# A low part by an adding DMA: how the FFN's last weights are split in two

## The chip, the cores and the metric

One core of a Trainium2 chip runs the whole kernel. The metric is the device time of one execution in microseconds; the time of a kernel is the median over runs.

## The reference

One layer of a streaming encoder on 512 tokens of width 1024, all in float32: RMSNorm, one wide projection, chunked attention with 16 heads beside a gated linear recurrence, a gated merge, then the feed-forward part and a last norm. The change sits in the last product of the feed-forward part:

```python
hn = rmsnorm(h, norm_ffn_g[l])
gu = hn @ w_ffn_in[l]                          # 1024 -> 2 x 2816
g, up = jnp.split(gu, 2, axis=-1)
h = h + (jax.nn.silu(g) * up) @ w_ffn_out[l]   # 2816 -> 1024
return rmsnorm(h, final_norm_g)
```

## The kernel before

The kernel multiplies in float32r (fp32r in the profile), so every float32 operand is split into a high part, which is the operand rounded to that format, and a low part, which is the operand minus the high part. A product is then three matmuls (`mm3`, lines 70 to 72): high by high, high by low, low by high. The split of a tile of weights is done by `split` (lines 76 and 77): ScalarE copies `raw` into the high part, VectorE subtracts the high part from `raw`. GpSimd does the subtraction in a few places only (lines 206, 839 and others).

Weights come in chunks, in an order that `plan` writes out. `load` issues a chunk's transfers from SP's queue into buffers tagged `raw`, each of 512 KB (128 partitions x 1024 float32); three of them rotate. `prefetch` splits each into a tile `hl` (named `whl_<chunk>` in the profile), which holds both parts; `weights(name, ahead)` makes that chunk and the next `ahead` of them. The chunks of `w_ffn_out` are named `fo<half>_<k0>`: two halves of the output columns (512 each), six chunks of rows each, five of 4x128 rows and a last one of 2x128. A chunk of 4 row blocks needs two tiles, the last one a single tile, so there are 22 tiles in all. Their `whl` buffers rotate in two groups of four: two chunks in the pool `wp`, which the earlier weights use too, then two in the pool `op` that is opened for this stage.

The feed-forward input projection (`fg` and `fu` chunks) is a Strassen-like product, `block_product`, whose last call is `fu20`; it prefetches `fo0_0`. Then, for the first half of the columns, the loop walks over chunks, and in each over the four blocks of 128 tokens (`out_tile`, four results side by side). The activations are split by `split_act` on the way, its low parts on GpSimd for pairs 0, 1, 2 and 4 and on VectorE for the others. The second half does the same for its first four chunks; its last two chunks are walked token block by token block, with the closing norm of each block behind it.

```python
wf = weights(f"fo{cc}_{k0}", 3)
for (t, at), po in zip(pieces, pos):
    out_tile(t, po, k0, wf, at)
```

The program gives the instructions in one order, and a planner that estimates durations at build time settles the order within each engine's queue. Each engine runs its own queue strictly in that order and waits on semaphores.

Of the kernel before, what the change touches and what calls it, by code (L numbers as in the profile page):

```python
# [10 lines left out]
AF = mybir.ActivationFunctionType  # L11
ALU = mybir.AluOpType
# [24 lines left out]
def block_kernel(ctx: ExitStack, tc: tile.TileContext, x, norm_mix_g, w_in, b_merge, rel_table,  # L37
# [3 lines left out]
    pe, dve, act, pool, sp = nc.tensor, nc.vector, nc.scalar, nc.gpsimd, nc.sync  # L41
# [20 lines left out]
    def f(ap):  # L62
        return ap.bitcast(F32)
# [10 lines left out]
    def split(hi, lo, src):  # L74

        act.activation(hi, src, AF.Copy)  # L76
        dve.tensor_sub(lo, src, f(hi))  # L77
# [55 lines left out]
    def load(name, k):  # L133
        _, parts, rows, kts = chunks[index[name]]
        wide = sum(width for *_, width in parts)
        n = min(4 * CW // wide, kts - k)
        at = rows + k * P
        pl, bufs = wp, 3
        if name in strassen and name[0] == "f":
            loads[0] += 1  # L140
            pl, bufs = (room[0], 1) if loads[0] % 4 == 0 else (wp, 3)
        raw = pl.tile([P, n, wide], F32, tag="raw", bufs=bufs, name=f"raw_{name}_{k}")
        to = 0
        for src, col, width in parts:
            sp.dma_start(out=raw[:, :, to:to + width],
                         in_=src[at:at + n * P, col:col + width].rearrange("(k p) e -> p k e", p=P))
            to += width
        raws[name, k] = raw
# [5 lines left out]
    def weight_sums(name):  # L154

        for k in (0, 4):
            if (name, k) not in raws:
                load(name, k)
        r0, r1 = raws.pop((name, 0)), raws.pop((name, 4))
        a11, a21, a12, a22 = r0[:, :, 0:P], r0[:, :, P:CW], r1[:, :, 0:P], r1[:, :, P:CW]  # L160
        sc = room[0]
        s21, s34 = (sc.tile([P, 2, 4, P], F32, tag=tag, bufs=1, name=f"{tag}_{name}")
                    for tag in ("s21", "s34"))
        s2, s1, s3, s4 = s21[:, 0], s21[:, 1], s34[:, 0], s34[:, 1]
        dve.tensor_add(s1, a21, a22)
        dve.tensor_sub(s2, s1, a11)
        other = pool if name in ("fg2", "fu2", "fg4") else dve
        other.tensor_sub(s3, a11, a21)
        other.tensor_sub(s4, a12, s2)
        blocks_ = {}  # L170
        for group in ((("a11", a11), ("a12", a12)), (("s2", s2), ("s1", s1)), (("s3", s3), ("s4", s4)), (("a22", a22),)):
            pl, tag, bufs = sc, "a22", 2
            if len(group) == 2:
                slots[0] += 1
                pl, tag, bufs = (sc, "whl", 1) if slots[0] % 5 == 0 else (wp, "whl", 4)
            o = pl.tile([P, len(group), 2, 4, P], F32R, tag=tag, bufs=bufs, name=f"whl_{name}_{group[0][0]}")
            together = group[0][0] in ("s2", "s3") and name != "fg2"
            if together:
                split(o[:, :, 0], o[:, :, 1], (s21 if group[0][0] == "s2" else s34)[:])
            for i, (key, src) in enumerate(group):  # L180
                if not together:
                    split(o[:, i, 0], o[:, i, 1], src)
                blocks_[key] = o[:, i]
        return blocks_

    def prefetch(n):
        while len(made) < min(n, len(chunks), index.get(barrier[0], len(chunks))):
            name, parts, rows, kts = chunks[len(made)]
            if name in strassen:
                made.append(weight_sums(name))  # L190
                continue
            tiles = []
            wide = sum(width for *_, width in parts)
            step = 4 * CW // wide
            for k in range(0, kts, step):
                n_ = min(step, kts - k)
                if name in extra:
                    hl = extra[name].tile([P, 2, n_, wide], F32R, tag="whl", bufs=4, name=f"whl_{name}_{k}")
                else:
                    hl = wp.tile([P, 2, n_, wide], F32R, tag="whl", bufs=4, name=f"whl_{name}_{k}")  # L200
                if (name, k) not in raws:
                    load(name, k)
                raw = raws.pop((name, k))
                if len(made) == 0 and k:
                    act.activation(hl[:, 0], raw[:], AF.Copy)
                    pool.tensor_sub(hl[:, 1], raw[:], f(hl[:, 0]))
                else:
                    split(hl[:, 0], hl[:, 1], raw[:])
                tiles.append(hl)
            made.append(lambda part, k, at, tiles=tiles, step=step: tiles[k // step][:, part, k % step, at])  # L210

    def weights(name, ahead=1):
        prefetch(index[name] + 1 + ahead)
        return made[index[name]]
# [70 lines left out]
    for name, w in (("r", w_rg_r), ("i", w_rg_i)):  # L285
        raw = nm.tile([P, 8, P], F32, name=f"wrg_raw_{name}")
# [146 lines left out]
    for name, raw in zip("ri", wrg_raw):  # L433
        hl = rw2.tile([P, 2, 8, P], F32R, bufs=1, name=f"wrg_{name}")
# [305 lines left out]

    hsq = []
    prefetch(index["wo1"] + 1)
    for t in range(NT):
        q2 = cp.tile([P, 2], F32, tag="hsq2", bufs=2, name=f"hsq2_{t}")
# [75 lines left out]
    room[0] = sc  # L820
    barrier[0] = "fo0_16"
    prefetch(index["fg2"] + 1)

    for i, name in enumerate(("fg0", "fg0", "fu0", "fu0")):
# [129 lines left out]
```

## Time and profile before

| | |
|---|---|
| median of 2 runs | 901.03 us (900.98 to 901.07) |
| the profiled execution | 900.88 us |
| its span | 899.1 us |
| mean granted TensorE clock | 0.993 |
| TensorE (PE) busy | 881.4 us |
| VectorE (DVE) busy | 553.6 us |
| ScalarE (ACT) busy | 473.5 us |
| GpSimd (POOL) busy | 133.1 us |

The span is what the profile covers; the execution's time has 1.8 us around it. A row of a group gives the line of the program, the engine, the operation, what is written and read, the number of instructions, their busy time in us and the mean of one in ns, then the idle time of that engine just ahead of them and what ended most of it. `SPq` is SP's queue, which issues DMAs.

### The profile page before, as it was taken

What the parts mean: (1) busy time and instruction counts of PE and PEld (TensorE: products, weight loads), DVE (VectorE), ACT (ScalarE), POOL (GpSimd) and SP (SyncE); (2) the same over time, 40 slices, a digit from 0 to 9 for tenths busy, and PEclk for the clock granted to TensorE, in tenths of its full rate; (3) what the DMA queues carried; (4) which work ended last, traced back from release to release, by engine and by line L of the source; (5) the groups of instructions that cost most, each with busy time, mean ns of one, the idle gap of its engine ahead of it and who ended that gap; (6) DMA issues with size and microseconds to landing.
All of it is one profiled execution on the core that took longest, in us unless ns stands there. A gap on an engine that the chain in (4) does not pass through costs nothing.

```text
span 899.1 us, 13343 instructions
## 1 busy us (share of the span) xinstructions
PE 881.4 (98%) x5220; PEld 778.1 (87%) x5220; DVE 553.6 (62%) x863; ACT 473.5 (53%) x841; POOL 133.1 (15%) x168
## 2 busy tenths in 40 slices
PE   8999999999999999999999999899999999999997
PEld 5988888888888889797888889899999999888886
DVE  5776556553466676666546455998888887453203
ACT  7566546642257666666533365556555556623103
POOL 4012112120023222222100002510000001300100
PEclk9999999999999999999999999899999999999999
DMA  8323222423332232331123620333433333353002
GB/s 261 95 71 117 85 84 90 118 94 94 105 104 73 74 111 64 93 95 60 66 63 124 217 66 30 117 117 95 140 96 94 96 118 108 98 184 120 30 1 94
DMA packets 85023, 89.05 MB, mean 99 GB/s; under 512 B 5344, under 2 KB 73552, under 8 KB 84960
## 3 DMA queue, kind: packets, MB, share of 16 engines
q1 hardware_dynamic: 83584, 84.73, 30.7%
q10 hardware_dynamic: 1376, 3.47, 1.1%
q8 instruction: 41, 0.67, 0.3%
q14 instruction: 22, 0.18, 0.1%
HBM read 86.05 MB, written 2.14 MB: 98 GB/s over the span
## 4 chain that ended last, share of the span: by engine, by line
PE 92%; DVE 3%; ACT 2%; issue 1%; DMA 1%; POOL 1%; SPq 0%; DVEq 0%; ACTq 0%; POOLq 0%
PE po_out L70 5%; PE po_out L72 5%; PE po_out L71 5%; PE p_fu L71 2%; PE p_fu L70 2%; PE p_fu L72 2%; PE p_fg L72 2%; PE p_fg L71 2%; PE p_fg L70 2%; PE o L659 2%; PE po_ga L70 2%; PE pT L639 2%; PE po_ga L71 2%; PE po_ga L72 2%; PE po_ya L70 2%; PE po_ya L71 2%
## 5 line engine op out<-in xcount | busy, mean ns | idle before, releaser
L70 PE MATMUL po_out<-whl_fo,act_hi 128*128 128x512 f32 (+1 forms) x198 | 73.2, 369 | 0.0
L71 PE MATMUL po_out<-whl_fo,act_hi 128*128 128x512 f32 (+1 forms) x198 | 72.9, 368 | 0.0
L72 PE MATMUL po_out<-whl_fo,act_lo 128*128 128x512 f32 (+1 forms) x198 | 72.1, 368 | 0.0
L77 DVE TENSOR_TENSOR whl_fo<-raw_fo,whl_fo 128x1024 fp32r<-128x1024 f32 x22 | 27.5, 1259 | 47.0 <-ACT whl_fo L76 47.0
L627 POOL TENSOR_SCALAR p<-p,rl 128x128 f32<-128x128 f32 (+1 forms) x64 | 37.4, 605 | 84.4 <-DVE rl L625 83.8
L76 ACT ACTIVATE whl_fo<-raw_fo 128x1024 fp32r<-128x1024 f32 x22 | 23.0, 1056 | 50.6 <-PE po_out L72 36.1
L624 ACT ACTIVATE p<-p,m 128x128 f32<-128x128 f32 (+3 forms) x64 | 35.5, 555 | 22.0 <-DVE m L623 21.6
L623 DVE CUSTOM_DVE_ANT_0 p<-s,bias 128x128 f32<-128x128 f32 (+3 forms) x64 | 29.8, 487 | 22.6 <-PE s L621 21.8
L72 PEld LDWEIGHTS po_out<-whl_fo,act_lo 128*128 128x128 f32 x198 | 37.2, 188 | 6.9
L70 PEld LDWEIGHTS po_out<-whl_fo,act_hi 128*128 128x128 f32 x198 | 37.2, 188 | 6.6
L71 PEld LDWEIGHTS po_out<-whl_fo,act_hi 128*128 128x128 f32 x198 | 37.2, 188 | 6.6
L659 PE MATMUL o<-pp,v 128*128 128x256 f32 (+2 forms) x128 | 35.4, 337 | 3.0 <-ACT pp L76 3.0
L839 POOL TENSOR_TENSOR act_lo<-act,act_hi 128x1024 fp32r<-128x1024 f32 x4 | 10.5, 2624 | 184.1 <-ACT act_hi L838 182.7
L71 PE MATMUL po_v<-whl_v,xnT 128*128 128x256 f32 x128 | 36.9, 288 | 0.0
L77 DVE TENSOR_TENSOR pp<-pT,pp 128x256 fp32r<-128x256 f32 (+2 forms) x64 | 30.4, 486 | 10.4 <-ACT pp L76 10.0
L70 PE MATMUL po_v<-whl_v,xnT 128*128 128x256 f32 x128 | 36.5, 285 | 0.0
L72 PE MATMUL po_v<-whl_v,xnT 128*128 128x256 f32 x128 | 36.4, 284 | 0.0
L76 ACT ACTIVATE pp<-pT 128x256 fp32r<-128x256 f32 (+2 forms) x64 | 26.5, 433 | 10.8 <-DVE pp L77 6.3
L77 DVE TENSOR_TENSOR whl_fu_s<-s_fu,whl_fu_s 128x1024 fp32r<-128x1024 f32 x20 | 25.3, 1280 | 5.7 <-ACT whl_fu_s L76 5.6
L71 PE MATMUL po_xr<-xnT,whl_xr 128*128 128x512 f32 (+1 forms) x80 | 27.9, 354 | 0.6 <-DVE xnT L327 0.5
L639 PE MATMUL pT<-ident,p 128*128 128x128 f32 x160 | 27.5, 273 | 0.7 <-POOL p L627 0.7
L70 PE MATMUL po_gr<-xnT,whl_gr 128*128 128x512 f32 (+1 forms) x80 | 27.8, 349 | 0.1
(354 smaller groups left out, 3089.9 us busy)
## 6 DMA issues: line engine op xcount, KB each, us to landing
raw_fg<-in_w_ffn_in_dram SPq DMA_DIRECT2D x22, 512.0 KB, 4.5
raw_fu<-in_w_ffn_in_dram SPq DMA_DIRECT2D x22, 512.0 KB, 3.6
raw_fo<-in_w_ffn_out_dram SPq DMA_DIRECT2D x22, 512.0 KB, 4.3
raw_qk<-in_w_in_dram SPq DMA_DIRECT2D x32, 256.0 KB, 3.3
raw_xr<-in_w_in_dram SPq DMA_DIRECT2D x8, 512.0 KB, 5.0
raw_gr<-in_w_in_dram SPq DMA_DIRECT2D x8, 512.0 KB, 3.5
raw_ga<-in_w_in_dram SPq DMA_DIRECT2D x8, 512.0 KB, 3.6
raw_gb<-in_w_in_dram SPq DMA_DIRECT2D x8, 512.0 KB, 3.7
```

The costliest lines, as they stand in the source:

```text
L70: pe.matmul(o, sh, mh, start=start, stop=False, skip_group_check=parts)
L71: pe.matmul(o, sh, ml, start=False, stop=False, skip_group_check=parts)
L72: pe.matmul(o, sl, mh, start=False, stop=stop, skip_group_check=parts)
L76: act.activation(hi, src, AF.Copy)
L77: dve.tensor_sub(lo, src, f(hi))
L623: dve.tensor_tensor_reduce(prob[qb][:], sc[:, 0:w], bias[:, S - w:S], -1.0, 3e38, ALU.add, ALU.min, nmax[:, qb:qb + 1])
L624: act.activation(prob[qb][:], prob[qb][:], AF.Exp, bias=nmax[:, qb:qb + 1], scale=-1.0, accum_out=lsum[:, qb:qb + 1])
L627: pool.tensor_scalar(prob[qb][:], prob[qb][:], rl[:, qb:qb + 1], 1.0, ALU.mult, ALU.mult)
L639: pe.transpose(pt[:, at * P:(at + 1) * P], prob[qb][:, kb * P:(kb + 1) * P], ident[:])
L659: pe.matmul(po[:, S - n:S], st, pp[i][:, part, lo:lo + n], start=kb == 0 and part == 0, stop=kb == NT - 1 and part == 1)
L839: (pool if i in (0, 1, 2, 4) else dve).tensor_sub(lo[:], o[:], f(hi[:]))
```

## The change

For the chunks whose name begins with `fo`, the low part is no longer subtracted on VectorE. ScalarE still copies `raw` to the high part. GpSimd multiplies `raw` by -1 into the place of the low part, where the result is rounded to the reduced format, so that it is the negated high part. Then a DMA, issued from GpSimd's queue, adds `raw` to it in place. The low part is ready when that transfer has landed, and `raw` may be loaded anew from then on. All other weights are split as before.

```diff
--- before.py
+++ after.py
@@ -204,6 +204,11 @@
                 if len(made) == 0 and k:
                     act.activation(hl[:, 0], raw[:], AF.Copy)
                     pool.tensor_sub(hl[:, 1], raw[:], f(hl[:, 0]))
+                elif name[:2] == "fo":
+
+                    act.activation(hl[:, 0], raw[:], AF.Copy)
+                    pool.tensor_scalar(hl[:, 1], raw[:], -1.0, None, ALU.mult)
+                    pool.dma_start(out=hl[:, 1], in_=raw[:], accum_op=ALU.add)
                 else:
                     split(hl[:, 0], hl[:, 1], raw[:])
                 tiles.append(hl)
```

## The prediction

> **What bounds the kernel now.** I read the page first, for the engine that sets the end.
>
> ```profile
> span 899.1 us, 13343 instructions
> PE 881.4 (98%) x5220; PEld 778.1 (87%) x5220; DVE 553.6 (62%) x863; ACT 473.5 (53%) x841; POOL 133.1 (15%) x168
> PE 92%; DVE 3%; ACT 2%; issue 1%; DMA 1%; POOL 1%; SPq 0%; DVEq 0%; ACTq 0%; POOLq 0%
> L77 DVE TENSOR_TENSOR whl_fo<-raw_fo,whl_fo 128x1024 fp32r<-128x1024 f32 x22 | 27.5, 1259 | 47.0 <-ACT whl_fo L76 47.0
> L76 ACT ACTIVATE whl_fo<-raw_fo 128x1024 fp32r<-128x1024 f32 x22 | 23.0, 1056 | 50.6 <-PE po_out L72 36.1
> ```
>
> TensorE is busy for 98% of the span and holds 92% of the chain that ended last. The 22 VectorE subtractions that the change removes (27.5 us in all) are in no row of that chain's leading groups, and VectorE itself idles 47.0 us in front of them. Next comes the view of one tile, for the weights concerned, and the busy time of each engine in the stretches where they are made.
>
> ```profile
> L70 PE MATMUL po_out<-whl_fo,act_hi x198: 277/394/399, 766.0 to 892.7; 128*128 128x512 f32 x154, 128*128 128x256 f32 x44
> L76 ACT ACTIVATE whl_fo<-raw_fo x22: 1038/1060/1064, 755.1 to 853.4; 128x1024 fp32r<-128x1024 f32 x22
> L77 DVE TENSOR_TENSOR whl_fo<-raw_fo,whl_fo x22: 1218/1225/2002, 756.2 to 854.5; 128x1024 fp32r<-128x1024 f32 x22
> ...
> 750.00:760.00 10.00, 10.00 (x86) 10.00 (x86) 8.20 (x10) 5.82 (x10) 0.48 (x1) 1.00 0.30 97
> 790.00:800.00 10.00, 10.00 (x45) 8.11 (x44) 6.85 (x7) 3.00 (x3) 0.00 (x0) 1.00 0.75 240
> sum 110.00, PE 110.00 PEld 95.42 DVE 54.77 ACT 48.64 POOL 16.55; mean PE 10.00 PEld 8.67 DVE 4.98 ACT 4.42 POOL 1.50
> ```
>
> The columns of the last three rows are the stretch, its length, then PE, PEld, DVE, ACT and POOL busy with their counts, granted clock, DMA share and GB/s; the sum runs over eleven stretches of 10 us from 740 to 850. TensorE fills 110.00 of 110.00 us at a granted clock of 1.00. So a faster VectorE can give nothing here: nobody on the path waits for it. The question is only whether the new way of making low parts is late for TensorE.
>
> **When each tile is needed.** There are 22 tiles of weights (two per chunk, one in the last chunk of each half), each 128x1024, and all that matters is the pace at which TensorE eats them.
>
> ```profile
> 766.03 0.40 PE L70 MATMUL po_out<-whl_fo,act_hi 128*128 128x512 f32 x1
> ...
> 769.01 0.28 PE L70 MATMUL p_fu<-bt,whl_fu_s 128*128 128x256 f32 x1
> ...
> 770.44 0.28 PE L70 MATMUL q_fu<-hn,whl_fu_s 128*128 128x256 f32 x1
> ...
> 772.99 0.28 PE L70 MATMUL p_fu<-bt,whl_fu_a 128*128 128x256 f32 x1
> ```
>
> The fo matmuls run from 766.0 to 892.7: 3 lines of 198, of which 3x154 are 512 wide and 3x44 are half that, so 528 full widths. Among the first of them stand 36 matmuls of the last fu product (12 each from 769.01, 770.44 and 772.99); the 750 to 760 row has 86 of that size in 10 us, so they take 4.2 us. The pace is (126.8 - 4.2)/528 = 0.232 us. A tile serves 4 token blocks x 2 rows of features x 3 matmuls = 24, so 5.57 us. Counting tiles from 0, tile 0 is needed at 766.0 and tile n at about 770.2 + 5.57n: tile 1 at 775.8, tile 3 at 786.9, tile 5 at 798.1. The last three (19 to 21) are all needed for the first token block of the final pass, from 770.2 + 19x5.57 = 876.0; tile 21 comes 12 matmuls later, at 878.8.
>
> **What it removes, adds and moves.** Removed: 22 subtractions on VectorE, 27.5 us, worth nothing on the path as shown. Kept: the ScalarE copy (high part), now beside the low part instead of ahead of it. Added, for each tile, on GpSimd: one negating pass over 128x1024 and one DMA issue; on the DMA engines: one transfer that reads 512 KB of raw and 512 KB of the negated part and writes 512 KB. Moved: the release of the raw buffer, from the end of the subtraction to the landing of that transfer; SP's next load of the same buffer (three in rotation) waits for it.
>
> ```profile
> L627 POOL TENSOR_SCALAR p<-p,rl 128x512 f32<-128x512 f32 x16 | 13.2, 828 | 0.0
> L627 POOL TENSOR_SCALAR p<-p,rl 128x128 f32<-128x128 f32 x16 | 6.9, 433 | 84.4 <-DVE rl L625 83.8
> L815 POOL TENSOR_TENSOR bt<-sum_t,bt 128x1024 fp32r<-128x1024 f32 x1 | 3.4, 3361 | 0.0
> ...
> L145 SPq DMA_DIRECT2D raw_fo<-in_w_ffn_out_dram x22: 367/368/368, 739.2 to 834.8; - x22
> ...
> raw_fo<-in_w_ffn_out_dram SPq DMA_DIRECT2D x22, 512.0 KB, 4.3
> h<-in_x_dram ACTq DMA_DIRECT2D x4, 512.0 KB, 7.3
> ...
> q1 hardware_dynamic: 6512, 12.06, 30.8%
> ```
>
> Negating pass: GpSimd's one-input rows rise by (828 - 433)/384 = 1.03 ns per column, so 828 + 512x1.03 = 1355 ns, 1.35 us. Issue on GpSimd: the profile has no DMA issued there. Below stands SP's issue, 0.37 us; above, the longest GpSimd instruction of this shape, 3.36 us. I take 1.35 us, as long as the one-input pass, since GpSimd must walk the same 128 partitions. The adding transfer: also unshown. From below, a plain load of 512 KB, 4.3 us; from above, two of the slowest 512 KB transfers, 2 x 7.3 = 14.6 us. I take 2 x 4.3 = 8.6 us, since two operands are read. The chain from a free buffer to a ready low part is then 1.35 + 1.35 + 8.6 = 11.3 us, against 1.06 + 1.23 = 2.3 us now.
>
> The Trainium skill ("Collectives: The Full Stack", The bandwidth ceiling) says that an add inside the DMA engine costs no time of its own, and that its second source read halves the rate; with the 2.0 us + bytes/436e3 of "DMA: Bandwidth & Descriptors" (Anatomy of one DMA) two reads come to an estimate of 2.0 + 2 x 1.2 = 4.4 us. By the rule the chain would be 7.1 us and never late; no run here shows it yet, and the sum keeps to the rows.
>
> Now the tiles in turn. The high-part copies show when buffers come free:
>
> ```profile
> 755.10 1.05 ACT L76 ACTIVATE whl_fo<-raw_fo 128x1024 fp32r<-128x1024 f32 x1
> ...
> 759.58 1.06 ACT L76 ACTIVATE whl_fo<-raw_fo 128x1024 fp32r<-128x1024 f32 x1 [1.02 <-PE q_fg L72]
> ...
> 763.80 1.04 ACT L76 ACTIVATE whl_fo<-raw_fo 128x1024 fp32r<-128x1024 f32 x1
> ...
> 802.46 1.06 ACT L76 ACTIVATE whl_fo<-raw_fo 128x1024 fp32r<-128x1024 f32 x1 [6.93 <-PE po_out L72]
> ...
> 813.63 1.06 ACT L76 ACTIVATE whl_fo<-raw_fo 128x1024 fp32r<-128x1024 f32 x1 [1.55 <-PE po_out L72]
> ...
> 772.10 4.91 POOL L839 TENSOR_TENSOR act_lo<-act,act_hi 128x1024 fp32r<-128x1024 f32 x2 [21.62 <-ACT act_hi L838]
> ```
>
> Tile 0: 755.1 + 11.3 = 766.4, needed at 766.0: 0.4 us late. Tile 1: 759.6 + 11.3 = 770.9 against 775.8. Tile 2: 775.1 against 781.3. From tile 3 on the three raw buffers bind: a buffer comes round after issue and load (0.37 + 4.3 = 4.67) and the chain (11.3), so every 16.0 us, 5.33 us per tile, a little under the 5.57 of TensorE. Tile 3: 766.4 + 16.0 = 782.4 against 786.9; tile 21, seven rounds after tile 0: 878.4 against 878.8. Weight buffers don't bind: eight rotate, so the fill of a chunk may start three chunks (33 us) ahead of its use; the releases by po_out at 802.46 and 813.63 are one chunk (11.2 us) apart, and 33 is thrice the chain.
>
> GpSimd's queue: the negation of tile 3 waits for raw data at 766.4 + 4.67 = 771.1, and the low part of the second activation pair (772.10) stands behind it; 771.1 + 2.7 = 773.8 would set that 1.7 us back, and TensorE wants it only at 775.8, after the 24 matmuls of tile 0. Total GpSimd work is 22 x 2.7 + 16.55 = 76 us of some 120. DMA engines: SP's queue took 30.8% of 121 us for 12.06 MB (739 to 860), so 1.62 us of all 16 engines for 0.524 MB; with an add of two such reads, 3 x 1.62 = 4.9 us per tile under 5.57.
>
> So the sum: removed 0, negation and issue 0 (hidden under TensorE), first tile +0.4, raw rotation 0. Against the profiled execution's own 900.9 us (span 899.1 and 1.8 around it; the runs' median is 901.0) that is **901.3 us**.
>
> **The rivals.** *The adding transfer is too slow (slower).* It decides from the point where a round of three raw buffers exceeds 3 x 5.57 = 16.7 us, that is an add above 9.3 us, and my 8.6 is close to it. At 14.6 us the chain is 17.3 and a round 22.0: tile 0 at 772.4, tile 21 at 772.4 + 154 = 926.4, 47.6 us late: 948.5. At 12 us a round is 19.4, tile 21 at 769.8 + 135.8 = 905.6: 927.7. For it: nothing in the trace shows an add by DMA, and the DMA share is already 0.75 in one stretch. Against: source and destination are both on the chip.
>
> *GpSimd's issue is the long part.* At the bound of 3.36 the chain is 13.3, a round 18.0, tile 21 at 768.4 + 126 = 894.4: +15.6, 916.5; halfway (2.35) a round is 17.0, and tile 21 at 767.4 + 119 = 886.4 gives +7.6, **908.5**. For it: GpSimd's time per instruction is the largest of all engines here. Against: it is idle for most of this stage (16.55 of 110 us busy), so only the latency counts.
>
> *A different instruction order.* The order of each queue is planned at build time, and new instructions move it. Between 766.0 and 774.4 fo and fu matmuls alternate; were fu's 36 placed first, tile 0 would be needed only at 770.2, and the 0.4 us vanish: 900.9. TensorE has no gap to win in this stage, and nothing before 739, where the first load of fo is issued, touches the edit. *The edit changes nothing in time* comes out at the same 900.9.
>
> **How the numbers follow.** No change (901.3 or 900.9, within about 2 us): 0.62. Slow issue or a start in the wrong order (903 to 917): 0.15. Slow add (905 to 949): 0.20. A lucky order, faster than 900: 0.03. Two per cent is 18 us, about what a measurement of this kernel can tell from no change: slower by that takes an end over 919, most of the slow-add case and the last of the slow-issue case, 0.18; faster by it has no mechanism, 0.01; within, 0.81. The range goes from 899.5 to 932; above it lies the upper third of the slow add, 0.07, below it 0.02.
>
> **What would show it.** Right: L77 no longer has whl_fo; GpSimd gains 22 one-input passes of about 1.35 us and 22 issues; TensorE still fills every 10 us from 770 to 890, first fo matmul near 766 to 771; the add lands within 9 us of issue; SP's loads wait on DMA instead of VectorE. Wrong: po_out rows with idle time in front, released by DMA whl_fo; an add above 9.3 us; a wider span in the stage alone, with loads of raw_fo spaced more than 5.6 us apart; GpSimd's issue over 2 us.

## The result and the profile after

| | before | after |
|---|---|---|
| median of 2 runs (lowest to highest) | 901.03 us (900.98 to 901.07) | 924.45 us (923.74 to 925.16) |
| ratio, 95% interval | | 1.026 (1.0216 to 1.0304) |
| the profiled execution, and its span | 900.88 us, 899.1 us | 925.16 us, 923.1 us |

The change makes the kernel slower by 23.4 us. The page of the kernel after, with the lines that answer to those shown of before:

```profile
span 923.1 us, 13395 instructions
PE 887.1 (96%) x5220; PEld 781.4 (85%) x5220; DVE 527.3 (57%) x841; ACT 473.7 (51%) x841; POOL 211.7 (23%) x212
PE 77%; DMA 9%; POOL 5%; DVE 3%; ACT 2%; issue 2%; SPq 0%; POOLq 0%; DVEq 0%; ACTq 0%
L71 PE MATMUL po_out<-whl_fo,act_hi 128*128 128x512 f32 (+1 forms) x198 | 76.1, 386 | 17.3 <-DMA whl_fo<-raw_fo 17.3
L210 POOL TENSOR_SCALAR whl_fo<-raw_fo 128x1024 fp32r<-128x1024 f32 x22 | 61.5, 2822 | 49.7 <-DMA raw_fo<-in_w_ffn_out_dram 43.7
whl_fo<-raw_fo POOLq DMA_DIRECT2D x22, 512.0 KB, 5.9
```

VectorE lost its 22 subtractions (863 to 841 instructions, 553.6 to 527.3 us), and nothing came of it. The chain that ended last, which was 92% TensorE, now holds 9% DMA and 5% GpSimd. Line 71 is the first matmul of the three that reads the low part; it waits 17.3 us for the adding DMA. The negating pass on GpSimd takes 2.82 us, twice its price.

The tile view and the same kernel's matmul stage as one stretch (stretch, length, then busy time of PE, PEld, DVE, ACT, POOL, granted clock, DMA share, GB/s):

```profile
L70 PE MATMUL po_out<-whl_fo,act_hi x198: 277/394/632, 764.6 to 916.2; 128*128 128x512 f32 x154, 128*128 128x256 f32 x44
...
DMA to landing us min/median/max: 4.5/5.9/11.1
...
764.00:917.00 153.00, 135.49 (x637) 111.81 (x635) 21.05 (x34) 39.67 (x55) 83.95 (x48) 0.93 0.61 146
```

The fo matmuls started from 766.0 to 892.7 before, and from 764.6 to 916.2 now: 126.7 us against 151.6. The difference of 24.9 us is all of the 24.0 by which the span grew, and 0.9 us more. TensorE is idle for 153.00 - 135.49 = 17.5 us of the last row's stretch. The other 7.4 us are in time that counts as busy. GpSimd's queue in order of time, and TensorE in stretches of 3 us, show where both come from:

```profile
803.13 8.24 POOL L210 TENSOR_SCALAR whl_fo<-raw_fo 128x1024 fp32r<-128x1024 f32 x3 [10.41 <-DMA raw_fo<-in_w_ffn_out_dram]
811.33 2.70 POOL L211 DMA_DIRECT2D whl_fo<-raw_fo  x3
823.87 8.24 POOL L210 TENSOR_SCALAR whl_fo<-raw_fo 128x1024 fp32r<-128x1024 f32 x3 [9.84 <-DMA raw_fo<-in_w_ffn_out_dram]
832.07 2.71 POOL L211 DMA_DIRECT2D whl_fo<-raw_fo  x3
```

```profile
806.00:809.00 3.00, 3.00 (x14) 2.44 (x13) 0.00 (x0) 0.84 (x1) 3.00 (x2) 1.00 0.03 5
809.00:812.00 3.00, 2.75 (x12) 1.88 (x10) 0.00 (x0) 0.00 (x0) 3.00 (x3) 1.00 0.00 0
812.00:815.00 3.00, 0.00 (x0) 0.00 (x0) 0.00 (x0) 0.00 (x0) 2.03 (x3) 0.89 0.83 153
815.00:818.00 3.00, 1.95 (x5) 1.56 (x6) 0.00 (x0) 0.00 (x0) 0.00 (x0) 0.50 1.04 197
818.00:821.00 3.00, 3.00 (x9) 2.32 (x8) 0.00 (x0) 0.00 (x0) 0.00 (x0) 0.50 1.04 153
821.00:824.00 3.00, 3.00 (x14) 2.48 (x13) 0.00 (x0) 0.21 (x1) 0.13 (x1) 0.97 1.00 332
```

GpSimd negates three tiles in a row, 8.24 us, and only then issues the three adds. While it negates, the DMA engines do nothing (shares of 0.03 and 0.00): all three raw buffers are waiting to be added. Once the adds are out, the DMA engines are full (1.04) and GpSimd idles for 9.84 us, until the next loads land. The two take turns instead of working side by side, and three tiles take 823.87 - 803.13 = 20.7 us, where TensorE eats them in 3 x 5.57 = 16.7. TensorE runs dry from 811.7 to about 816. The first matmuls after that run at a granted clock of 0.50: 9 in 3 us, where the row of 806 to 809 has 14. Summed over stretches of 1 us, the clock below full speed takes 7.0 of the 7.4 us.

These are TensorE's five waits for an add, with the length of each in brackets:

```profile
794.76 0.50 PE L71 MATMUL po_out<-whl_fo,act_hi 128*128 128x512 f32 x1 [2.57 <-DMA whl_fo<-raw_fo]
816.05 0.79 PE L71 MATMUL po_out<-whl_fo,act_hi 128*128 128x512 f32 x1 [4.31 <-DMA whl_fo<-raw_fo]
836.75 0.50 PE L71 MATMUL po_out<-whl_fo,act_hi 128*128 128x512 f32 x1 [0.71 <-DMA whl_fo<-raw_fo]
859.95 0.80 PE L71 MATMUL po_out<-whl_fo,act_hi 128*128 128x512 f32 x1 [6.91 <-DMA whl_fo<-raw_fo]
888.59 0.50 PE L71 MATMUL po_out<-whl_fo,act_hi 128*128 128x512 f32 x1 [2.77 <-DMA whl_fo<-raw_fo]
```

Read in stretches of 0.25 us, the clock is at 0.50 for 6.8 us with the wait of 4.31 (from 814.3 to 821.2), for 10.2 us with that of 6.91 and for 3.4 us with that of 2.77; the waits of 2.57 and 0.71 cost no clock. The Trainium skill ("TensorE: Matmul & The Clock Gate", What's actually happening) has the clock halve after one idle window of some 3.4 us and come back after as long a busy one. The trace agrees in the unit, for the three stretches are two, three and one times 3.4 us, but not in the idle time needed: the clock fell some 2.6 us after the last matmul before the wait of 4.31, and a wait of 2.77 us was enough where one of 2.57 was not.

### The profile page after: what moved, and what is told of

It reads as the page before. It is cut to its first block, busy times and chain, and to the rows that moved or that the text cites. A ratio compares the mean times of both kernels' runs of the same rounds, so it can differ in the third digit from the quotient of the medians.

```text
span 923.1 us, 13395 instructions
## 1 busy us (share of the span) xinstructions
PE 887.1 (96%) x5220; PEld 781.4 (85%) x5220; DVE 527.3 (57%) x841; ACT 473.7 (51%) x841; POOL 211.7 (23%) x212
## 4 chain that ended last, share of the span: by engine, by line
PE 77%; DMA 9%; POOL 5%; DVE 3%; ACT 2%; issue 2%; SPq 0%; POOLq 0%; DVEq 0%; ACTq 0%
DMA whl_fo<-raw_fo 5%; POOL whl_fo L210 3%; DMA raw_fo<-in_w_ffn_out_dram 3%; PE p_fg L72 2%; PE p_fg L70 2%; PE p_fg L71 2%; PE p_fu L71 2%; PE p_fu L70 2%; PE p_fu L72 2%; PE o L664 2%; PE pT L644 2%; PE po_ya L70 2%; PE po_ya L71 2%; PE po_yb L71 2%; PE po_yb L70 2%
## 5 line engine op out<-in xcount | busy, mean ns | idle before, releaser
L71 PE MATMUL po_out<-whl_fo,act_hi 128*128 128x512 f32 (+1 forms) x198 | 76.1, 386 | 17.3 <-DMA whl_fo<-raw_fo 17.3
L72 PE MATMUL po_out<-whl_fo,act_lo 128*128 128x512 f32 (+1 forms) x198 | 74.4, 382 | 0.0
L210 POOL TENSOR_SCALAR whl_fo<-raw_fo 128x1024 fp32r<-128x1024 f32 x22 | 61.5, 2822 | 49.7 <-DMA raw_fo<-in_w_ffn_out_dram 43.7
L882 DVE TENSOR_TENSOR h<-po_out,h 128x512 f32<-128x512 f32 (+1 forms) x9 | 5.5, 625 | 105.5 <-PE po_out L72 105.5
L71 PEld LDWEIGHTS po_out<-whl_fo,act_hi 128*128 128x128 f32 x198 | 38.9, 196 | 26.2 <-DMA whl_fo<-raw_fo 19.2
L70 PEld LDWEIGHTS po_out<-whl_fo,act_hi 128*128 128x128 f32 x198 | 38.5, 195 | 7.2
L806 POOL TENSOR_TENSOR sum_t<-x,x 128x512 f32<-128x512 f32 x2 | 3.6, 1783 | 116.8 <-ACT x L334 116.8
```

The source lines that it names most:

```text
L70: pe.matmul(o, sh, mh, start=start, stop=False, skip_group_check=parts)
L71: pe.matmul(o, sh, ml, start=False, stop=False, skip_group_check=parts)
L72: pe.matmul(o, sl, mh, start=False, stop=stop, skip_group_check=parts)
L210: pool.tensor_scalar(hl[:, 1], raw[:], -1.0, None, ALU.mult)
```

## The experiments

Theory A: the order in GpSimd's queue, negations in batches ahead of their issues, is the loss. B: the transfers themselves are too much for the DMA engines. C: the long negation is. All ratios are to the kernel before on the same chip, with 95% intervals.

**Pairs.**

```diff
- pool.tensor_scalar(hl[:, 1], raw[:], -1.0, None, ALU.mult)
- pool.dma_start(out=hl[:, 1], in_=raw[:], accum_op=ALU.add)
+ with ExitStack() as behind:
+     if issued:
+         behind.enter_context(tc.issue_after(issued[-1]))
+     pool.tensor_scalar(hl[:, 1], raw[:], -1.0, None, ALU.mult)
+ issued.append(pool.dma_start(out=hl[:, 1], in_=raw[:], accum_op=ALU.add).ins)
```

> Each negation is queued on GpSimd behind the adding DMA of the tile before, so the order is negate, issue, negate, issue. Theory A (batches): the loss comes from three negations in a row (8.24 us) ahead of three issues, in which the DMA engines idle, so three tiles take 20.7 us where TensorE eats them in 16.7; in pairs a buffer comes round after 2.8 + 1.0 + some 5 + some 4.5 = 13 to 14 us: 901 to 906 us. Theory B (transfer): loads and adds fill the DMA engines, three adds side by side land after 10 to 11 us, and the order doesn't matter: 920 to 926 us. Theory C (long negation): GpSimd's 2.77 us, twice what was forecast, is the loss itself: stays at 918 or more.

Measured: 903.36 us, ratio 1.002 (1.0011 to 1.0030). Same instructions, same bytes, same buffers as the change, and 21 of its 23 us are gone. GpSimd's queue and the sum over stretches of 10 us from 740 to 890:

```profile
795.85 2.76 POOL L214 TENSOR_SCALAR whl_fo<-raw_fo 128x1024 fp32r<-128x1024 f32 x1 [2.20 <-DMA raw_fo<-in_w_ffn_out_dram]
799.03 0.91 POOL L215 DMA_DIRECT2D whl_fo<-raw_fo  x1 [0.42 <-POOL whl_fo L214]
799.66 3.12 POOL L214 TENSOR_SCALAR whl_fo<-raw_fo 128x1024 fp32r<-128x1024 f32 x1
803.18 0.91 POOL L215 DMA_DIRECT2D whl_fo<-raw_fo  x1 [0.41 <-POOL whl_fo L214]
...
800.00:810.00 10.00, 10.00 (x44) 8.08 (x43) 0.00 (x0) 1.67 (x2) 7.42 (x4) 1.00 0.95 217
sum 150.00, PE 150.00 PEld 129.70 DVE 37.24 ACT 52.06 POOL 96.06; mean PE 10.00 PEld 8.65 DVE 2.48 ACT 3.47 POOL 6.40
```

TensorE fills 150 of 150 us, though a negation still takes 2.76 us or more. Now GpSimd (7.42 of 10 us) and the DMA engines (0.95) work at the same time. The adds land after 5.4 us at the median and 7.1 at the most. B and C are out as causes by themselves.

**ScalarE negates.**

```diff
- pool.tensor_scalar(hl[:, 1], raw[:], -1.0, None, ALU.mult)
+ act.activation(hl[:, 1], raw[:], AF.Copy, scale=-1.0)
```

> The negation goes to ScalarE (a copy with scale -1, about 1.06 us as the high part's copy), GpSimd only issues the adding DMA. A: nothing stands between the issues, no batches, 901 to 905 us. B: the adds are the same size and number, 918 to 926 us. C: 901 to 905 us.

Measured: 901.52 us, ratio 1.0002 (0.9992 to 1.0013), no difference from before. GpSimd has no negation to put ahead of its issues, so no batch can form in its queue. A and C both expected this; B did not.

**A copy in place of the add.**

```diff
- pool.dma_start(out=hl[:, 1], in_=raw[:], accum_op=ALU.add)
+ pool.dma_start(out=hl[:, 1], in_=raw[:])
```

> The DMA copies raw over the negated part and adds nothing (the addition is left out); order and number of instructions on GpSimd stay. One read in place of two: the transfer's engine time falls from 3.1 us to about 1.6 us per tile. A: the round of three shrinks from 20.7 by some 4.5 to 16 us, near the 16.7 of TensorE: 902 to 910 us. B: the transfer was the bound, 901 to 906 us. C: the negations stay, 915 or more.

Measured: 904.14 us, ratio 1.0031 (1.0019 to 1.0044). The kernel leaves the addition out. TensorE still waits once for the copy, 1.7 us. The negations stay and the loss nearly goes, so C is out again; A and B both expected this.

**Six raw buffers.**

```diff
+ if name in extra and name[:2] == "fo":
+     pl = extra[name]
```

`extra[name]` is the pool `op`, in which three more buffers tagged `raw` rotate.

> Chunks 2, 3, 6, 7, 10 and 11 load their raw tiles into three buffers of their own, so six rotate in place of three; nothing else changes. A: while three buffers are negated, the other three load or are added to, and the DMA engines no longer idle: 901 to 908 us. B: same bytes through the same engines: 918 to 926 us. C: 915 or more.

Measured: 921.38 us, ratio 1.0219 (1.0203 to 1.0234): a miss for A as I had put it, and the figure that B and C wanted. GpSimd's queue and TensorE in this run:

```profile
785.05 14.89 POOL L212 TENSOR_SCALAR whl_fo<-raw_fo 128x1024 fp32r<-128x1024 f32 x5 [4.43 <-DMA raw_fo<-in_w_ffn_out_dram]
799.88 1.79 POOL L213 DMA_DIRECT2D whl_fo<-raw_fo  x2
...
790.00:800.00 10.00, 2.11 (x10) 1.38 (x8) 0.00 (x0) 0.90 (x1) 10.00 (x5) 0.86 0.00 0
...
804.52 0.80 PE L71 MATMUL po_out<-whl_fo,act_hi 128*128 128x512 f32 x1 [12.40 <-DMA whl_fo<-raw_fo]
...
815.07 0.80 PE L71 MATMUL po_out<-whl_fo,act_hi 128*128 128x512 f32 x1 [3.41 <-DMA whl_fo<-raw_fo]
...
860.00:870.00 10.00, 10.00 (x52) 8.39 (x52) 0.00 (x0) 2.01 (x2) 7.64 (x5) 1.00 0.68 129
```

More raw tiles were ready, and the queue was built with five negations ahead of the next issue: two waits of TensorE, 12.4 and 3.4 us, in place of five, with the DMA engines at 0.00 from 790 to 800. From 820 on TensorE is full. So buffers don't mend an order; whether they do harm by themselves needed a run of its own.

**Pairs and six buffers** (both edits above).

> The pairs (negate, issue, negate, issue) together with six raw buffers. Theory A (batches): the six raw buffers alone were no help because GpSimd's queue then negates five tiles (14.9 us) ahead of the first issue; with the order mended 901 to 903 us. Rival D (more transfers in flight disturb each other): six buffers cost by themselves, 912 us or more.

Measured: 902.91 us, ratio 1.0027 (1.0015 to 1.0040). The buffers do no harm, and no good: in pairs, three were enough.

**Twos.** The adds of a chunk are issued together, behind both of its negations, and the next chunk's negations come behind them.

```diff
- pool.tensor_scalar(hl[:, 1], raw[:], -1.0, None, ALU.mult)
- pool.dma_start(out=hl[:, 1], in_=raw[:], accum_op=ALU.add)
+ with ExitStack() as behind:
+     if issued:
+         behind.enter_context(tc.issue_after(issued[-1]))
+     last = pool.tensor_scalar(hl[:, 1], raw[:], -1.0, None, ALU.mult)
+ pend.append((hl, raw))
...
+ with tc.issue_after(last.ins):
+     for hl, raw in pend:
+         d = pool.dma_start(out=hl[:, 1], in_=raw[:], accum_op=ALU.add)
```

> GpSimd's order is forced to two negations, then two issues, a chunk at a time; three raw buffers. A: a cost between pairs (903.4) and batches of three (924.4): two negations of 2.8 us, an issue, two adds of 3.1 us of engine time side by side and a load come to 5.5 + 0.9 + 2 + 6.2 + 3.5 = some 18 us for two buffers, with the third one working in the gap, against 3 x 5.57: 904 to 914 us. If only the number of buffers and bytes counted: 903, as the pairs.

Measured: 910.01 us, ratio 1.0110 (1.0091 to 1.0128). TensorE has six waits for adds, each under 1 us (3.9 in all), and the clock stays at 1.00. Batches of one tile, of two and of up to three: 903.4, 910.0 and 924.4 us. The loss grows with the batch.

**A cast in place of the negation.**

```diff
- pool.tensor_scalar(hl[:, 1], raw[:], -1.0, None, ALU.mult)
+ pool.tensor_copy(hl[:, 1], raw[:])
```

> GpSimd copies raw with rounding in place of multiplying by -1 (the sign is left out, so the transfer adds raw to plus the high part); the batches of three stay. The 64x512 casts of the kernel took 657 ns, so about 1.3 us for 1024 columns against 2.77. A with the length of the negation as a factor: a round of three falls from 20.7 by 3 x 1.45 to 16.3 us, just under TensorE's 16.7: 901 to 907 us. If the batch costs whatever the negation takes: 915 or more.

Measured: 902.62 us, ratio 1.0022 (1.0011 to 1.0033). The tile view, and the queue in one batch:

```profile
L210 POOL CAST whl_fo<-raw_fo x22: 1032/1042/1976, 754.1 to 870.1; 128x1024 fp32r<-128x1024 f32 x22
...
796.72 1.04 POOL L210 CAST whl_fo<-raw_fo 128x1024 fp32r<-128x1024 f32 x1 [10.38 <-DMA raw_fo<-in_w_ffn_out_dram]
...
813.78 1.04 POOL L210 CAST whl_fo<-raw_fo 128x1024 fp32r<-128x1024 f32 x1 [10.70 <-DMA raw_fo<-in_w_ffn_out_dram]
...
817.38 2.67 POOL L211 DMA_DIRECT2D whl_fo<-raw_fo  x3
```

The sign is left out, and the batches of three are all there, but a pass takes 1.04 us; the issues follow 3.6 us after the batch's start instead of 8.2, and TensorE waits only 0.1 us in all. The time is as expected, the round is not: from 796.72 to 813.78 it takes 17.1 us, where 16.3 was expected, and the next three take 17.4 to 18.4. So 16.7 us is no sharp limit: the four rounds run over it by some 4 us in all, and as far as these sums show, the tiles made ahead cover that. The loss takes both, batches and a round well above 16.7; a shorter pass (here) or a shorter transfer (the copy) brings the round down without touching the order.

**GpSimd subtracts, no DMA.**

```diff
- pool.tensor_scalar(hl[:, 1], raw[:], -1.0, None, ALU.mult)
- pool.dma_start(out=hl[:, 1], in_=raw[:], accum_op=ALU.add)
+ pool.tensor_sub(hl[:, 1], raw[:], f(hl[:, 0]))
```

> GpSimd subtracts the high part from raw itself (about 2.5 us a tile, behind ScalarE's copy), with no DMA: raw is free again when GpSimd is done. A: GpSimd's time per tile is under TensorE's 5.57 us, 901 to 902 us. If GpSimd as the maker of low parts were the loss: 910 or more.

Measured: 900.64 us, ratio 1.0000 (0.9987 to 1.0013). GpSimd may well make the low parts; with no DMA behind its pass the loss is gone. It is no gain either, since TensorE is the bound.

**Two operations in the negation.**

```diff
- pool.tensor_scalar(hl[:, 1], raw[:], -1.0, None, ALU.mult)
+ pool.tensor_scalar(hl[:, 1], raw[:], -1.0, 1.0, ALU.mult, ALU.mult)
```

> The negation is written with two scalar operations (times -1, times 1) as the rows it was priced from are; the planner then puts most negations and issues in pairs by itself (one batch of three is left), so the time is expected near the pairs, 902 to 906 us, whatever the negation costs. What it tells is the negation's duration: 1.35 us if the form with one operation was the slow part of 2.77 us, 2.7 us or more if the rounded output is.

Measured: 902.91 us, ratio 1.0021 (1.0010 to 1.0032). Its tile view, and the queue at one tile:

```profile
L210 POOL TENSOR_SCALAR whl_fo<-raw_fo x22: 1037/1058/2009, 752.8 to 864.9; 128x1024 fp32r<-128x1024 f32 x22
...
812.47 1.04 POOL L210 TENSOR_SCALAR whl_fo<-raw_fo 128x1024 fp32r<-128x1024 f32 x1 [8.72 <-DMA raw_fo<-in_w_ffn_out_dram]
813.92 0.87 POOL L211 DMA_DIRECT2D whl_fo<-raw_fo  x1 [0.41 <-POOL whl_fo L210]
```

The same pass with a needless second operation takes 1.06 us in place of 2.77. With it the change costs 2 us instead of 23, but not by the pass alone: the order differs too. Most negations are followed by their own issue, as in these rows; one batch of three and some of two are left. This run can't tell the shorter pass from the order. The cast, which kept the batches, and the pairs, which kept the pass, can.

## Why the prediction was right in part

The range (899.5 to 932.0) holds 924.45; the forecast of no change (901.3) was wrong. That the range holds is luck: its upper part stands for a slow add and a slow issue, and neither is what cost the time.

Right: TensorE was the bound, and removing 27.5 us from VectorE brought nothing. Right too: the ways out of "no change" all went through the rotation of raw buffers, with the limit of 16.7 us for a round of three (roughly, as the cast showed), and the wrong signs that I named came (line 71 idle, released by DMA whl_fo).

The step that failed is "a buffer comes round after issue and load (0.37 + 4.3 = 4.67) and the chain (11.3), so every 16.0 us". It let each buffer run its own circle, with one pass of 1.35 us in it. By the rows above, a round of 20.7 us is 8.2 us of negations (803.13 to 811.33), three in a row at twice the price each, and 12.5 us for issue, add and load together (811.33 to 823.87), for which the prediction had 14.6. A tile's own terms were not too small in sum: a negation of 2.77 (priced 1.35), an issue of about 0.9 (priced 1.35) and an add that lands in 5.9 at the median (priced 8.6) make 9.6 us, less than 11.3. In pairs, where each buffer does run its own circle, the time is 903.4, near the forecast. In the kernel as built the three circles were in step: a tile waits for two more negations before its own add is even issued, and three adds at once land up to 11.1 us after issue.

Of the rivals, the one on instruction order was the right mechanism in the wrong queue. I priced a new order of TensorE's matmuls, at 900.9, and never asked in which order GpSimd would hold 22 negations and 22 issues, though GpSimd is the engine that got them. The slow add (905 to 949, chance 0.20) comes out at the right size for another reason. Its premise, an add above 9.3 us, holds only for the last of several adds in flight (11.1 at the most here, 7.1 in pairs); the shortest landed in 4.5 us. For that shortest one the Trainium skill's rules gave 4.4 us as an estimate ("Collectives: The Full Stack", The bandwidth ceiling, with "DMA: Bandwidth & Descriptors", Anatomy of one DMA), better than my 8.6 from rows. The engine time of an add was well sized: the adding queue of the kernel after, from 803.5 to 824,

```profile
q0 software_dynamic: 432, 1.57, 45.4%
```

moved three adds in 45.4% of 20.5 us, 3.1 us each against the 2 x 1.62 of the sum. The slow issue named GpSimd, but the wrong instruction: the issue took 0.9 us where I had 1.35, for which no row stood, and the negation was the long part. The negation's 1.35 us was drawn from rows whose instructions have two scalar operations; in that form it takes 1.06.

The drop of TensorE's clock with three of the five waits, 7.0 us of the loss, was in no step of the forecast.

What stays open: why the queue was built with negations first was not tried, only what that order costs; and where the 2 us come from that the pairs keep against before. They are not in this stage: in the profiled execution of the pairs the fo matmuls start from 767.0 to 893.7, 126.7 us as before.

## What to carry to other kernels

When work moves to another engine and a DMA, ask in which order that engine's queue will hold the new instructions: a pass and the issue that follows it belong in pairs, for here the engine that did three passes first left the DMA engines idle and turned a rotation of buffers into lockstep. Check the round of the buffers for the batch, not for one tile, before adding buffers; six here instead of three made a batch of five. And a wait of TensorE can cost more than its length: three of the five here halved its clock for 3.4 to 10.2 us.

## What the runs showed of the hardware

A scalar multiplication on GpSimd over 128x1024, float32 to float32r, took 2.77 us with one operation and 1.06 us with a second one (times 1); a cast of the same shape took 1.04 us. An adding DMA of 512 KB inside SBUF landed 4.5 us after issue at the least and took 3.1 us of all 16 engines; its issue held GpSimd for about 0.9 us. TensorE's clock was halved for 3.4, 6.8 and 10.2 us with waits of 2.77, 4.31 and 6.91 us, and not with waits of 2.57 us and less.
